# Index keys of a sparse attention kept twice, padded with zeros, so that one product of 128 rows and 512 columns serves two heads

## The chip, the cores and the metric

The kernel runs on one core of a Trainium2 chip. The metric is the time of one execution on the device, in microseconds (us), lower is better. The core has five engines with a queue of instructions each: TensorE (PE, matrix products; its weight loads are listed as PEld), VectorE (DVE), ScalarE (ACT), GpSimd (POOL) and SyncE (SP, which issues the transfers from memory). Each works through its own queue in order, and they wait for one another by semaphores.

## The reference

Two layers with three sublayers each: a feed-forward, a mixer, a feed-forward. For 256 tokens of width 1024, each sublayer computes `x <- LayerNorm(alpha * x + (1 + gate) * f(x * (1 + scale) + shift))`. The mixer of the first layer joins a sparse attention with a gated delta rule. The sparse attention has an index that picks the keys which each query may see:

```python
dots = jnp.einsum('bqhd,bsd->bqhs', iqb, ik32) * IDX_DIM ** -0.5     # 8 index heads of 64, one key of 64 for all
score = jnp.einsum('bqh,bqhs->bqs', iwb, jax.nn.relu(dots))          # weighted sum over the heads
score = jnp.where(visible, score, NEG_INF)
_, sel = lax.top_k(score, top_k)                                     # the 64 best keys of each query
```

The delta rule needs, for each chunk of 64 tokens and each of 4 heads, the inverse of a triangular matrix, and then carries a state from chunk to chunk.

## The kernel before

The tokens lie in two blocks of 128 (`NB`). Weights are split into a high and a low part, and a product of weights and activations is three products in fp32r (`mm3`, L263 to L265). Products inside the mixer, those of the index among them, are in plain float32.

The class `Hybrid` holds the mixer of the first layer. Its `run` projects in turn z, the index key and the gates' inputs (`use_ik`), and the queries, keys and values of the delta rule. Then comes `gdn`, the delta rule: its inversion goes up by levels (L1269 to L1284), with the two token blocks in turn. Each level multiplies on PE (L1272), copies the product to SBUF on ACT (L1274), and multiplies twice more (L1277 and L1281), after which DVE subtracts from the inverse so far (L1282, L1284). Behind it, in the program's text, come the index queries (`use_iq`) and `index`.

For each block, `index` multiplies the 128 queries of a head with the 256 keys. A head has 64 rows, so two heads lie above each other in `iqT` (128 rows, four pairs). The key stands twice in `ikd`, in rows 0 to 63 and in rows 64 to 127, so that each of the two heads has it in its own half of the array (L1060). Two pairs fill two PSUM banks of 512 columns, one bank for the upper heads and one for the lower. ACT takes the Relu of a bank (L1064), DVE multiplies by the head's weight and adds (L1068), and then finds the 64th best score in eight steps (L1072, L1073) and turns it into a bias (L1075, L1076).

A scheduler orders the instructions of each engine ahead of time: it lays instructions that are ready between those that wait, so that products of the index and of later projections stand between those of the delta rule. It also decides which semaphores an instruction waits for. A tile in SBUF can lie where an earlier tile lay; its first writer then waits for the last users of the earlier one. Tiles of the mixer are allocated one behind the other in the pools `hyb` and `hyb1`.

Two more places matter. `gates` (L1134) takes the exponential of `alog`, which is loaded from memory, into the tile `gea`; ACT has to load the table of this function first. And `epilogue` closes the sublayer ahead of the mixer: it normalises x in pieces on ACT (L405) and DVE (L407), PE transposes them (L282), ACT and DVE scale, shift and split the result (L298, L258, L259) into `uT`, and `uT` is what the z projection multiplies first.

Of the kernel before, what the change touches and what calls it, by code (L numbers as in the profile page):

```python
# [11 lines left out]
F32 = mybir.dt.float32  # L12
F32R = mybir.dt.float32r
I32 = mybir.dt.int32
AF = mybir.ActivationFunctionType
ALU = mybir.AluOpType
AX = mybir.AxisListType

P = 128
D = 1024  # L20
KD = D // P
S = 256
# [11 lines left out]
class Trunk:  # L34
# [804 lines left out]
    def run(self, subs):  # L839
        nc = self.nc  # L840
        self.subs = subs
        self.mdone = set()
        self.count = 0
        self.marks, self.last_mm = [None], None
        self.left = None
        goals = (44, 64, 98, 132, 136, 144)
        self.setup()
        self.lead = 0
        self.bg = self.mod_gen()
        self.need(0, 1)  # L850
        self.count += next(self.bg)
        todo = self.todo = [self.sublayer(si, l, j) for si, (l, j) in enumerate(subs)]
        self.make_u(0, self.x, range(NB))
        self.rest = self.setup_rest()
        for si, (l, j) in enumerate(subs):
            last = si == len(subs) - 1
            self.lead = 2 if j == 1 else 0
            self.si, self.base, self.goal = si, self.count, goals[si]
            for _ in todo[si]:
                pass  # L860
            self.need(si, 2)
            self.early, self.gb = [], None
            if not last:
                self.need(si + 1, 0)
                next(todo[si + 1])
            self.load_gb(l, j)
            self.epilogue(si, self.acc, last)
            self.left = self.residual()
            if not last and self.gb is None and subs[si + 1] != (0, 1):
                with self.behind(*self.marks):  # L870
                    for _ in self.left:
                        pass
# [42 lines left out]
class Hybrid:  # L915
# [19 lines left out]
    def run(self):  # L935
        T, nc, one, pool, w = self.T, self.nc, self.one, self.pool, self.w
        zs = T.proj_tok(self.wz, 512, True)
        with T.behind(*T.marks):
            self.constants()
        self.ikd = one.tile([P, S], F32, name="ikd")  # L940
        self.iw = one.tile([P, NB, 8], F32, name="iw")
        self.ab = one.tile([P, NB, 8], F32, name="ab")
        T.proj_t(pool, w, (2048, 72, 3656, 8), 80, self.use_ik)
        gates = self.gates(zs)
        next(gates)
        self.qkv = {}
        for i in range(6):
            if i == 1:
                with T.behind(self.T.recent):
                    for _ in T.left:  # L950
                        pass
            if i == 3:
                for _ in gates:
                    pass
            T.proj_t(pool, w, 2120 + 256 * i, 256, self.use_qkv, (None, nc.gpsimd))
        self.gdn()
        self.iqT = self.tl(one, [P, 4, S], "iqT")
        for i in range(2):
            T.proj_t(pool, w, 1536 + 256 * i, 256, self.use_iq, (nc.gpsimd,))
        self.index()  # L960
        self.aqT = self.tl(one, [P, 4, S], "iqT")
        self.akT = one.tile([P, 4, S], F32, name="akT")
        self.av = one.tile([P, NB, 8, self.DH], F32, name="av")

        def part(g):
            T.proj_t(pool, w, 256 * g, 256, self.use_aq, (nc.gpsimd,))
            self.beat()
            T.proj_t(pool, w, 512 + 256 * g, 256, self.use_ak, (nc.gpsimd,))
            self.beat()
            pts = T.proj_tok(T.tok_load(pool, w, 1024 + 256 * g, 256), 256, False)  # L970
            for b in range(NB):
                nc.scalar.copy(self.av[:, b, 4 * g : 4 * g + 4].rearrange("p h d -> p (h d)"), pts[b][:, 0:256])
            self.beat()

        part(0)
        first = self.dsa(0)
        part(1)
        mix = self.tl(T.wp, [P, 2, KD, S], "uT", F32R)
        op = OutProj(T, pool, "hl", 4, T.t["hyb_w_out"][0], mix)
        self.gdn_out(mix)  # L980
        T.attended(pool, *first, mix, 0)
        second = self.dsa(1, {0: (4,), 1: (5,), 2: (6, 7), 3: (0, 1)}, op)
        T.attended(pool, *second, mix, 2)
        with T.behind(T.turned):
            T.preload(AF.Silu, second[1][:, 1, 3:4])
        for k in (2, 3):
            op.ready(k)
        op.finish(HYBRID_LATE, (2, 3))
        return op.acc
# [25 lines left out]
    def use_ik(self, c, pt):  # L1015
        nc, T = self.nc, self.T
        kw = self.tl(self.pool, [P, S], "k1", bufs=4)
        nc.scalar.copy(kw[0:80], pt[0:80])
        nc.vector.tensor_copy(self.ikd[0:64], pt[0:64])
        nc.vector.tensor_copy(self.ikd[64:128], pt[0:64])  # L1020
        for b in range(NB):
            p2 = T.bank("acc")
            nc.tensor.transpose(p2[:, 0:80], kw[0:80, b * P : (b + 1) * P], T.ident[0:80, 0:80])
            nc.vector.tensor_scalar_mul(self.iw[:, b], p2[:, 64:72], 8.0 ** -0.5)
            nc.vector.tensor_copy(self.ab[:, b], p2[:, 72:80])
# [24 lines left out]
    def index(self):  # L1050
        nc, T = self.nc, self.T
        self.bias = []
        for b in range(NB):
            sc = self.tl(self.one, [P, S], f"sc{b}")
            for hq in range(2):
                pts = [T.bank("acc") for _ in range(2)]
                for i in range(2):
                    for r in range(2):
                        rr = slice(64 * r, 64 * r + 64)
                        nc.tensor.matmul(pts[r][:, i * S : (i + 1) * S], self.iqT[rr, 2 * hq + i, b * P : (b + 1) * P],  # L1060
                                         self.ikd[rr], start=True, stop=True)
                for r in range(2):
                    rl = self.tl(self.pool, [P, 512], "PT")
                    nc.scalar.activation(rl, pts[r], AF.Relu, scale=0.125)  # L1064
                    for i in range(2):
                        h = 4 * hq + 2 * i + r
                        wc = self.iw[:, b, h : h + 1]
                        nc.vector.scalar_tensor_tensor(sc, rl[:, i * S : (i + 1) * S], wc, T.mneg[b] if h == 0 else sc,  # L1068
                                                       ALU.mult, ALU.add)
            for _ in range(8):  # L1070
                m8 = self.tl(self.pool, [P, 8], "m8")
                nc.vector.max(m8, sc)  # L1072
                nc.vector.match_replace(sc, m8, sc, -3e38)  # L1073
            bias = sc
            nc.vector.tensor_scalar(bias, sc, -2e38, NEG, ALU.is_gt, ALU.mult)  # L1075
            nc.vector.tensor_tensor(out=bias, in0=bias, in1=T.nd[b], op=ALU.add)  # L1076
            self.bias.append(bias)
# [460 lines left out]
```

## Time and profile before

| | |
|---|---|
| time of three runs | 1206.98 us median, 1205.5 to 1210.03 |
| profiled execution | 1209.47 us, its span 1207.7 us |
| granted clock of PE, mean | 0.982 |
| PE busy | 94% of the span, 7703 instructions |
| DVE busy | 76% |
| ACT busy | 45% |
| POOL busy | 21% |
| index products, L1060 | 32 instructions of 428 ns, 333.4 to 359.3 us |

Times in the profile count from the start of the span. A matmul's record holds its way through the array, so records of neighbours overlap, and a busy PE is not a PE at its peak. The index and the inversion of the delta rule fill the stretch from 333 to 363 us; the epilogue ahead of the mixer runs from 224 to 245 us.

### The profile page before, as it was taken

What the parts mean: (1) busy time and instruction counts of PE and PEld (TensorE: products, weight loads), DVE (VectorE), ACT (ScalarE), POOL (GpSimd) and SP (SyncE); (2) the same over time, 40 slices, a digit from 0 to 9 for tenths busy, and PEclk for the clock granted to TensorE, in tenths of its full rate; (3) what the DMA queues carried; (4) which work ended last, traced back from release to release, by engine and by line L of the source; (5) the groups of instructions that cost most, each with busy time, mean ns of one, the idle gap of its engine ahead of it and who ended that gap; (6) DMA issues with size and microseconds to landing.
All of it is one profiled execution on the core that took longest, in us unless ns stands there. A gap on an engine that the chain in (4) does not pass through costs nothing.

```text
span 1207.7 us, 19560 instructions
## 1 busy us (share of the span) xinstructions
PE 1131.0 (94%) x7703; PEld 1025.9 (85%) x7703; DVE 917.7 (76%) x1404; ACT 548.5 (45%) x963; POOL 259.4 (21%) x186
## 2 busy tenths in 40 slices
PE   4998999998899998999999999999989998999997
PEld 3887999788787887989999899898988877899995
DVE  6699777698986677878775889767789748866545
ACT  0645444456433445543543543434347656544430
POOL 0631000224731452320000342000122234300001
PEclk9998999999999999999999899999989999999999
DMA  9879998453310576789987488888733335885620
GB/s 354 266 252 342 299 327 299 139 179 119 97 36 5 188 270 218 238 293 320 311 298 248 134 284 283 270 278 298 250 122 102 139 105 190 294 253 185 211 71 35
DMA packets 155333, 259.74 MB, mean 215 GB/s; under 512 B 8813, under 2 KB 117354, under 8 KB 155242
## 3 DMA queue, kind: packets, MB, share of 16 engines
q1 hardware_dynamic: 155050, 258.45, 64.4%
q8 instruction: 60, 0.98, 0.3%
q14 instruction: 31, 0.25, 0.1%
q10 hardware_dynamic: 192, 0.05, 0.0%
HBM read 257.43 MB, written 1.05 MB: 214 GB/s over the span
## 4 chain that ended last, share of the span: by engine, by line
PE 51%; DVE 23%; DMA 13%; issue 5%; ACT 4%; POOL 3%; SPq 0%; POOLq 0%; DVEq 0%; ACTq 0%
PE gu L265 8%; PE gu L263 8%; PE gu L264 8%; PE acc L265 6%; PE acc L264 6%; PE acc L263 6%; DMA wd<-ffn_w_down 5%; DMA wd<-mod_w 4%; DVE macc L225 3%; DMA w<-ffn_w_up 2%; DVE g L259 2%; DVE x L383 1%; POOL hd L259 1%; DMA w<-mod_w 1%; DVE u L259 1%
## 5 line engine op out<-in xcount | busy, mean ns | idle before, releaser
L225 DVE SCALAR_TENSOR_TENSOR macc<-wd,csT,macc 128x1024 f32<-128x1024 f32 x112 | 171.5, 1531 | 28.6 <-DMA wd<-mod_w 28.0
L265 PE MATMUL gu<-uT,g 128*128 128x256 f32 x640 | 181.3, 283 | 1.6 <-DVE g L259 1.6
L263 PE MATMUL gu<-uT,g 128*128 128x256 f32 x640 | 181.2, 283 | 1.3 <-ACT sg L548 1.3
L265 PE MATMUL gu<-uT,u 128*128 128x256 f32 x640 | 181.3, 283 | 1.0 <-DVE u L259 1.0
L263 PE MATMUL gu<-uT,u 128*128 128x256 f32 x640 | 181.2, 283 | 0.0
L264 PE MATMUL gu<-uT,u 128*128 128x256 f32 x640 | 181.1, 283 | 0.0
L264 PE MATMUL gu<-uT,g 128*128 128x256 f32 x640 | 181.1, 283 | 0.0
L258 ACT CAST hd<-wd 128x1024 fp32r<-128x1024 f32 x88 | 92.3, 1049 | 136.8 <-DMA wd<-ffn_w_down 118.8
L263 PE MATMUL acc<-hd,h 128*128 128x512 f32 x352 | 141.5, 402 | 0.5 <-ACT h L258 0.5
L265 PE MATMUL acc<-hd,h 128*128 128x512 f32 x352 | 138.0, 392 | 1.8 <-DVE h L259 1.8
L264 PE MATMUL acc<-hd,h 128*128 128x512 f32 x352 | 138.1, 392 | 0.0
L259 DVE TENSOR_TENSOR g<-w,g 128x1024 fp32r<-128x1024 f32 x86 | 117.0, 1364 | 23.9 <-ACT g L258 23.8
L263 PEld LDWEIGHTS gu<-uT,g 128*128 128x128 f32 x640 | 122.7, 192 | 3.2 <-ACT sg L548 1.8
L265 PEld LDWEIGHTS gu<-uT,g 128*128 128x128 f32 x640 | 122.7, 192 | 2.2 <-DVE g L259 2.2
L264 PEld LDWEIGHTS gu<-uT,g 128*128 128x128 f32 x640 | 122.7, 192 | 1.4
L265 PEld LDWEIGHTS gu<-uT,u 128*128 128x128 f32 x640 | 122.9, 192 | 1.2 <-DVE u L259 1.2
L264 PEld LDWEIGHTS gu<-uT,u 128*128 128x128 f32 x640 | 122.9, 192 | 0.0
L263 PEld LDWEIGHTS gu<-uT,u 128*128 128x128 f32 x640 | 122.9, 192 | 0.0
L259 DVE TENSOR_TENSOR u<-w,u 128x1024 fp32r<-128x1024 f32 x81 | 106.6, 1321 | 20.1 <-ACT u L258 20.0
L259 POOL TENSOR_TENSOR hd<-wd,hd 128x1024 fp32r<-128x1024 f32 x32 | 89.6, 2806 | 137.9 <-ACT hd L258 137.9
L258 ACT CAST u<-w 128x1024 fp32r<-128x1024 f32 (+1 forms) x89 | 91.7, 1038 | 58.1 <-DMA w<-ffn_w_up 44.8
L259 POOL TENSOR_TENSOR hl<-w,hl 128x1024 fp32r<-128x1024 f32 x28 | 72.5, 2602 | 202.0 <-ACT hl L258 201.5
(403 smaller groups left out, 2477.6 us busy)
## 6 DMA issues: line engine op xcount, KB each, us to landing
wd<-mod_w SPq DMA_DIRECT2D x130, 512.0 KB, 4.8
wd<-ffn_w_down SPq DMA_DIRECT2D x88, 512.0 KB, 4.6
w<-ffn_w_gate SPq DMA_DIRECT2D x43, 1024.0 KB, 8.4
w<-ffn_w_up SPq DMA_DIRECT2D x43, 1024.0 KB, 6.3
w<-hyb_w_in SPq DMA_DIRECT2D x16, 1024.0 KB, 6.1
w<-mod_w SPq DMA_DIRECT2D x7, 1024.0 KB, 7.5
w<-hyb_w_out SPq DMA_DIRECT2D x4, 1024.0 KB, 5.0
w<-mla_w_out SPq DMA_DIRECT2D x4, 1024.0 KB, 5.1
```

What stands on the lines that cost most here:

```text
L225: step = nc.vector.scalar_tensor_tensor(acc, w, c, acc, ALU.mult, ALU.add)
L258: i = self.nc.scalar.copy(hi, src)
L259: return i, (eng or self.nc.vector).tensor_tensor(out=lo, in0=src, in1=hi.bitcast(F32), op=ALU.subtract)
L263: nc.tensor.matmul(out, lh, rh, start=first, stop=False)
L264: nc.tensor.matmul(out, lh, rl, start=False, stop=False)
L265: self.last_mm = nc.tensor.matmul(out, ll, rh, start=False, stop=last)
L383: V.tensor_tensor(out=x[:, b, sl], in0=tmp, in1=x[:, b, sl], op=ALU.add)
```

## The change

The key tile becomes `ik2`, twice as wide: its first 256 columns hold the key in rows 0 to 63 and zeros below, its second 256 columns hold zeros above and the key in rows 64 to 127. POOL writes the zeros once. A product now takes all 128 rows of a pair of heads and all 512 columns, and its result has the upper head in the first half of one bank and the lower head in the second half. There is one product for each pair and block, a Relu behind each, and the heads are added in the order 0 to 7.

```diff
-        self.ikd = one.tile([P, S], F32, name="ikd")
+        self.ik2 = one.tile([P, 2, S], F32, name="ik2")
+        for r in range(2):
+            nc.gpsimd.memset(self.ik2[64 - 64 * r : 128 - 64 * r, r], 0.0)
...
-        nc.vector.tensor_copy(self.ikd[0:64], pt[0:64])
-        nc.vector.tensor_copy(self.ikd[64:128], pt[0:64])
+        nc.vector.tensor_copy(self.ik2[0:64, 0], pt[0:64])
+        nc.vector.tensor_copy(self.ik2[64:128, 1], pt[0:64])
...
-            for hq in range(2):
-                pts = [T.bank("acc") for _ in range(2)]
-                for i in range(2):
-                    for r in range(2):
-                        rr = slice(64 * r, 64 * r + 64)
-                        nc.tensor.matmul(pts[r][:, i * S : (i + 1) * S], self.iqT[rr, 2 * hq + i, b * P : (b + 1) * P],
-                                         self.ikd[rr], start=True, stop=True)
+            for p in range(4):
+                pt = T.bank("acc")
+                nc.tensor.matmul(pt, self.iqT[:, p, b * P : (b + 1) * P], self.ik2.rearrange("p a b -> p (a b)"),
+                                 start=True, stop=True)
+                rl = self.tl(self.pool, [P, 512], "PT")
+                nc.scalar.activation(rl, pt, AF.Relu, scale=0.125)
                 for r in range(2):
-                    rl = self.tl(self.pool, [P, 512], "PT")
-                    nc.scalar.activation(rl, pts[r], AF.Relu, scale=0.125)
-                    for i in range(2):
-                        h = 4 * hq + 2 * i + r
...
+                    h = 2 * p + r
...
```

On PE, in the inversion, the order before is this; L1060 stands for one product of 64 rows, and two of them, one for each half of the array, follow each other between L1272 and L1277.

```order
L1060 MATMUL acc_3740<-ikd,iqT_3618 128x256
L1060 MATMUL acc_3741<-ikd,iqT_3618 128x256
L1277 MATMUL gu_3338<-decT_488_3336,tok_480_3303 128x128 x4
L1281 MATMUL gu_3343<-tok_480_3303,decT_488_3336 128x128 x4
L1272 MATMUL gu_3352<-dec_476_3291,vn_3350 128x128 x4
L1060 MATMUL acc_3740<-ikd,iqT_3618 128x256
L1060 MATMUL acc_3741<-ikd,iqT_3618 128x256
L1277 MATMUL gu_3359<-decT_493_3357,tok_477_3292 128x128 x4
```

In the changed kernel the same place reads as follows; its lines are numbered two less here, so L1059 is the index product, and L1275, L1279 and L1270 are the former L1277, L1281 and L1272.

```order
L1059 MATMUL acc_3742<-ik_2510,iqT_3620 128x512
L1275 MATMUL gu_3340<-decT_488_3338,tok_480_3305 128x128 x4
L1279 MATMUL gu_3345<-tok_480_3305,decT_488_3338 128x128 x4
L1270 MATMUL gu_3354<-dec_476_3293,vn_3352 128x128 x4
L1059 MATMUL acc_3748<-ik_2510,iqT_3620 128x512
L1275 MATMUL gu_3361<-decT_493_3359,tok_477_3294 128x128 x4
```

One product of 128 rows and 512 columns stands where the pair stood, in each of the eight rounds; the products around it are the same in the same order.

On ACT, at the end of the feed-forward ahead of the mixer, the order before has the table load free of waits; the names in brackets are the queues whose semaphores an instruction waits for, DMAHW6_49 being that of the transfer of `alog`.

```order
L258 CAST hl_2322<-w_296_2320 128x1024 [waits DMAHW5_49]
L258 CAST hl_2325<-w_296_2320 128x1024
L1134 ACT_TABLE_LOAD
L1134 ACTIVATE gea_2595<-alog 128x4 [waits DMAHW6_49]
L405 ACTIVATE x_118<-x_118,rs_2342 128x256 [waits DVE_49]
L405 ACTIVATE x_118<-x_118,rs_2342 128x256
```

In the changed kernel the same six instructions stand in the same order (L1132 is the former L1134).

```order
L258 CAST hl_2322<-w_296_2320 128x1024 [waits DMAHW5_49]
L258 CAST hl_2325<-w_296_2320 128x1024
L1132 ACT_TABLE_LOAD [waits DMAHW6_49,DVE_49]
L1132 ACTIVATE gea_2597<-alog 128x4 [waits PE_49]
L405 ACTIVATE x_118<-x_118,rs_2342 128x256 [waits DVE_49]
L405 ACTIVATE x_118<-x_118,rs_2342 128x256
```

The wait for the transfer has moved from the exponential to the table load ahead of it, and two waits have come, for DVE and PE instructions of the feed-forward.

On DVE, at the end of the inversion, the order before is this; `sc_563` and `sc_580` are the scores of the first and the second token block, `dec_476` and `dec_479` the inverses of the two blocks.

```order
L1068 SCALAR_TENSOR_TENSOR sc_580_3794<-PT_3815,iw,sc_580_3794 128x256
L1282 TENSOR_TENSOR dec_476_3291<-dec_476_3291,gu_3485 128x512
L1075 TENSOR_SCALAR sc_563_3739<-sc_563_3739 128x256
L1068 SCALAR_TENSOR_TENSOR sc_580_3794<-PT_3819,iw,sc_580_3794 128x256
L1076 TENSOR_TENSOR sc_563_3739<-sc_563_3739,nd_956 128x256
L1068 SCALAR_TENSOR_TENSOR sc_580_3794<-PT_3819,iw,sc_580_3794 128x256
L1072 MAX m_589_3823<-sc_580_3794 128x8
L1282 TENSOR_TENSOR dec_479_3302<-dec_479_3302,gu_3500 128x512
```

And in the changed kernel (again two lines less):

```order
L1066 SCALAR_TENSOR_TENSOR sc_580_3792<-PT_3813,iw,sc_580_3792 128x256
L1280 TENSOR_TENSOR dec_476_3293<-dec_476_3293,gu_3487 128x512
L1073 TENSOR_SCALAR sc_563_3741<-sc_563_3741 128x256
L1066 SCALAR_TENSOR_TENSOR sc_580_3792<-PT_3813,iw,sc_580_3792 128x256
L1074 TENSOR_TENSOR sc_563_3741<-sc_563_3741,nd_956 128x256
L1070 MAX m_589_3817<-sc_580_3792 128x8
L1071 MATCH_REPLACE sc_580_3792<-m_589_3817,sc_580_3792 128x256
L1070 MAX m_590_3820<-sc_580_3792 128x8
L1280 TENSOR_TENSOR dec_479_3304<-dec_479_3304,gu_3502 128x512
```

Between the last two subtractions from the inverse there is one accumulation of scores less, and one step of the search more.

## Rows read from the trace of the kernel before

**Rows 1.** The page: busy time, share of the span and instructions of each engine.
```profile
PE 1131.0 (94%) x7703; PEld 1025.9 (85%) x7703; DVE 917.7 (76%) x1404; ACT 548.5 (45%) x963; POOL 259.4 (21%) x186
```

**Rows 2.** The chain of waits from 333 us: start us, length us, what.
```profile
333.44 0.63 PE acc L1060 x4
...
337.04 0.59 ACT decT L1274
337.68 1.16 PE gu L1277 x8
...
340.71 0.59 ACT decT L1274
```

**Rows 3.** Timeline of PE, second round: start us, length, engine, line, operation, tiles, count.
```profile
336.67 0.28 PE L1272 MATMUL gu<-dec,vn 128*128 128x128 f32 x1
336.87 0.49 PE L1060 MATMUL acc<-ikd,iqT 64*128 64x256 f32 x2
337.19 0.38 PE L1060 MATMUL acc<-ikd,iqT 64*128 64x256 f32 x2
337.68 0.38 PE L1277 MATMUL gu<-decT,tok 128*128 128x128 f32 x1
```

**Rows 4.** Index products by line (busy us, mean ns); L180 in the timeline.
```profile
L1060 PE MATMUL acc<-ikd,iqT 64*128 64x256 f32 x32 | 5.6, 428 | 0.0
...
401.76 0.59 PE L180 MATMUL gu<-macc,one 128*128 128x512 f32 x1
401.76 1.02 PE L180 MATMUL gu<-macc,one 128*128 128x512 f32 x2
```

**Rows 5.** End of the inversion in the timeline; the search's maximum by line.
```profile
364.74 0.67 DVE L1282 TENSOR_TENSOR dec<-dec,gu 128x512 f32<-128x512 f32 x1
365.46 0.97 PEld L1289 LDWEIGHTS gu<-vb,dec 128*128 128x128 f32 x8 [0.20 <-DVE dec L1282]
...
L1072 DVE MAX8 m<-sc 128x8 f32<-128x256 f32 x16 | 6.8, 426 | 0.4
```

**Rows 6.** POOL by line (a fill, a copy); timeline of PE and POOL near 222 us.
```profile
masks.py:197 POOL MEMSET ident<- 128x128 f32 x1 | 0.2, 204 | 0.3 <-POOLq L1527 0.3
...
L1456 POOL COPY kt<-rkT 64x256 f32<-64x256 f32 x8 | 5.0, 676 | 0.1
...
221.50 0.39 PE L265 MATMUL acc<-hd,h 128*128 128x512 f32 x1
...
223.44 5.23 POOL L259 TENSOR_TENSOR hl<-w,hl 128x1024 fp32r<-128x1024 f32 x2 [127.47 <-ACT hl L258]
```

**Rows 7.** Timeline of the epilogue ahead of the mixer; in brackets idle time before, and releaser.
```profile
225.28 1.28 ACT L1134 ACT_TABLE_LOAD   x1
...
234.60 0.21 ACT L1134 ACTIVATE gea<-alog 128x4 f32<-128x4 f32 x1 [8.04 <-DMA alog<-gdn_a_log]
...
235.27 1.09 ACT L405 ACTIVATE x<-x,rs 128x256 f32<-128x256 f32 x2 [0.46 <-DVE rs L400]
...
235.92 1.15 PE L282 MATMUL gu<-ident,x 128*128 128x128 f32 x8 [1.80 <-ACT x L405]
...
237.90 0.50 PE L263 MATMUL acc<-hl,uT 128*128 128x512 f32 x1 [0.83 <-ACT uT L258]
...
239.89 0.76 DVE L259 TENSOR_TENSOR uT<-v,uT 128x256 fp32r<-128x256 f32 x2
...
240.37 0.51 PE L265 MATMUL acc<-hl,uT 128*128 128x512 f32 x1 [0.22 <-DVE uT L259]
```

**Rows 8.** Windows: length, busy us of PE, PEld, DVE, ACT, POOL, PEclk, DMA share, GB/s.
```profile
237.00:240.00 3.00, 2.17 (x9) 1.35 (x8) 2.22 (x9) 3.00 (x10) 0.82 (x2) 1.00 1.04 261
...
676.00:680.00 4.00, 2.24 (x13) 1.92 (x14) 3.23 (x12) 2.86 (x9) 0.81 (x2) 0.95 0.42 131
680.00:684.00 4.00, 3.44 (x17) 3.14 (x16) 2.20 (x7) 2.23 (x6) 0.00 (x0) 0.50 0.01 4
684.00:688.00 4.00, 4.00 (x26) 4.00 (x25) 3.46 (x7) 3.89 (x9) 0.58 (x1) 0.70 0.00 0
```

More of the change, by code (lines that the diff above doesn't have):

```diff
@@ L1054, in index @@
             sc = self.tl(self.one, [P, S], f"sc{b}")
-            for hq in range(2):
-                pts = [T.bank("acc") for _ in range(2)]
-                for i in range(2):
-                    for r in range(2):
-                        rr = slice(64 * r, 64 * r + 64)
-                        nc.tensor.matmul(pts[r][:, i * S : (i + 1) * S], self.iqT[rr, 2 * hq + i, b * P : (b + 1) * P],
-                                         self.ikd[rr], start=True, stop=True)
-                for r in range(2):
-                    rl = self.tl(self.pool, [P, 512], "PT")
-                    nc.scalar.activation(rl, pts[r], AF.Relu, scale=0.125)
-                    for i in range(2):
-                        h = 4 * hq + 2 * i + r
-                        wc = self.iw[:, b, h : h + 1]
-                        nc.vector.scalar_tensor_tensor(sc, rl[:, i * S : (i + 1) * S], wc, T.mneg[b] if h == 0 else sc,
-                                                       ALU.mult, ALU.add)
+            for p in range(4):
[4 more added lines that the diff above has]
+                nc.scalar.activation(rl, pt, AF.Relu, scale=0.125)
+                for r in range(2):
+                    h = 2 * p + r
+                    wc = self.iw[:, b, h : h + 1]
+                    nc.vector.scalar_tensor_tensor(sc, rl[:, r * S : (r + 1) * S], wc, T.mneg[b] if h == 0 else sc,
+                                                   ALU.mult, ALU.add)
             for _ in range(8):
```

## Prediction

> **What bounds the kernel now.** I read the page first: TensorE (PE) is busy 94% of the span [rows 1]. A share over the whole span does not say what the changed lines are worth, so I went to the chain of waits over the stretch where they run, 333 to 363 us. In that chain the reader is to see a pattern that comes back every 3.67 us: L1277, L1281 and L1272 on PE, then a copy on ScalarE (ACT, L1274, 0.59 us), then L1277 again [rows 2]. This is the inversion in the delta rule, in which each product needs the copy of the one before. The index products of L1060 stand in the chain once only, in the first round, for 0.63 us; in the other seven rounds their place is taken by the copy. So they run in the hole that PE has while ACT copies.
>
> The timeline of PE in steps of 0.05 us shows that hole in the second round [rows 3]. The last of L1272 starts at 336.67. L1060 follows at 336.87, two instructions together (0.49 us for both), and two more at 337.19 that end at 337.57. L1277 could not come sooner than its 337.68, since it needs the copy, which the chain has from 337.04 to 337.63 [rows 2]. A float32 product is two instructions here, so one group is two products of 64 rows, one in each half of the array, side by side: each instruction lasts 0.43 us [rows 4], but four take 0.70 us and not 1.7.
>
> **The change part by part.** *The product.* Eight groups of two half-array products (32 instructions) become eight products of 128 rows and 512 columns (16 instructions). The trace has that shape in L180: one instruction takes 0.59 us and two take 1.02, so they follow each other at 0.43 us [rows 4]. So a group grows from 0.70 to 1.02 us, and over eight groups PE's records grow by 8 x 0.32 = 2.6 us. The change does not halve PE's work, it adds to it, because the two halves already ran at the same time.
>
> Here a rule speaks against the change. The Trainium skill, page "TensorEngine Tiling (Array Packing)", section "The Solution", lets a contraction of at most 64 rows run as two independent tiles, up to twice as fast; padding with zeros gives that up. The two starts together in [rows 3] agree with it. The same page, section "Key Properties", says that changing the tiling mode drains TensorE, which speaks for the change; what that would give is the fourth rival.
>
> What of the 2.6 us is on the path? The new product starts at 336.78 if it follows L1272 as instructions of one form do (0.11 us apart: L1277's eight take 1.16 us [rows 2], the first alone 0.38 [rows 3], which leaves 0.78 for seven steps), else at 336.87. Its two instructions hold the array for 2 x 0.43 us, to 337.64 or 337.73. L1277 begins at 337.68 with its weights, and its first product, recorded 0.10 us longer than the others (0.38 against 0.28 us), really streams from about 337.78. So the hole holds it, with 0.05 to 0.14 us to spare. In seven rounds I put it at 0; the ends are 0 (the copy bounds the round, so nothing is gained) and 0.32 us a round, 2.2 us. In the first round L1060 is on the chain, and 0.63 becomes 0.86 us less the 0.08 us by which it starts sooner: +0.15 us.
>
> *ScalarE and VectorE in the index.* The counts and shapes stay: eight Relus of 512 columns, sixteen accumulations of 256. Only their order moves: a Relu now follows each product instead of two after every second one. Each stands ahead of a copy L1274 in ACT's queue, and that could hold up the chain; but the product ends at about 337.9, the Relu 0.6 us later, and the next copy on ACT starts at 340.71 [rows 2], over 2 us later. VectorE (DVE) finishes the first block's scores sooner, and at the end of the inversion this counts a little: L1282 started at 364.74, behind index work, and PE's L1289 waited 0.20 us for it [rows 5]. In the new order the second block's accumulations run one product ahead, and a search step stands in their place; the L1282 of the round before, and with it this one, should come sooner. I take -0.20 us, the whole wait; the other end is +0.4, if the search step only comes on top (its maximum alone is 0.43 us [rows 5]).
>
> *The zeros.* Two fills of 64x256 on GpSimd (POOL). The nearest rows are a fill of 128x128 (0.20 us) and a copy of 64x256 (0.68 us) [rows 6], so both together take 0.4 to 1.4 us. They wait for a product near the end of the feed-forward, the second of five tiles in the first bank, which ends at 221.9, and ahead of them POOL had been idle for 127 us. Behind them is the split of the z weights, which started at 223.44 only when ACT had cast [rows 6]. The gap is 1.5 us: cost 0. At the upper end, with no cover, it is the start of the z projection, at 237.9, that would move, which the 5.2 us of splits leave 9 us free.
>
> *Memory.* The keys take 1 KB more in each partition, so every tile allocated after them in that pool moves. Everywhere but once the waits stay what they were. The exception is gea (L1134, the decay rates): it now lies on a place that the feed-forward used, so its instruction has two waits more, and two of its three were put on the table load in front of it. Before, the table load ran at 225.28, with ACT otherwise idle, and only gea waited until 234.60 for the transfer of a_log [rows 7]. Now the table load itself waits for that transfer, and its 1.28 us come after it: 234.60 + 1.28 + 0.2 = 236.08. Behind it on ACT is L405, the normalising of x at the end of the feed-forward, which started at 235.27: 0.8 us late. For L405 PE's transposes wait (L282, idle 1.80 us [rows 7]), and for ACT's next casts the z projection (idle 0.83 us). So PE's first z product moves from 237.90 to 238.7. Not all of this lasts: six products later, at 239.52 and now 240.32, come two more of 0.23 us, then one that began at 240.37 because it waited 0.22 us for DVE's uT of 239.89. That uT stands on DVE behind work which is not late, so it does not move; the product now starts at 240.78, 0.41 us later than before. From there to 247.9 PE waits for nothing. I take +0.41 us. The ends are 0 (the table load is not held back) and 0.8.
>
> *Elsewhere.* SyncE issues the same transfers in the same order. In the delta rule's state steps six fill-in products move from the waits of the chain to a later place where PE is full: PE does the same work, 0.
>
> Sum: +0.15 - 0.20 + 0.41 = **+0.36 us**. The profiled execution took 1209.47 us (span 1207.7), 2.5 us over the median of 1206.98; on it the sum gives 1209.8, on the median **1207.3 us**. No change that can be measured: 0.5%, about what a measurement of this kernel can tell from none, is 6.0 us.
>
> **The rivals.** *The pause in the epilogue drops PE's clock (slower).* In the epilogue of another sublayer the granted clock was 0.95 while PE was busy 2.24 of 4 us, and then 0.50 and 0.70 for 4 us each, half speed for much of them [rows 8]. From 237 to 240 PE is busy 2.17 of 3 us, and the clock is at 1.00. The change makes exactly this pause 0.8 us longer. It decides if the clock falls before the z products, which then go at 1.2 GHz. The price is what full speed lost there: 4 x 0.50 + 4 x 0.30 = 3.2 us, so 1207.3 + 3.2 = 1210.5 us. For it: the pattern is the same. Against it: with PE's waits of 1.80 and 0.83 us [rows 7] the clock held, and 0.8 us more is a part of that. The Trainium skill, page "TensorE: Matmul & The Clock Gate", section "Why this matters for your kernels", warns of idle gaps between bursts for this reason; the 0.50 after the busy 2.24 agrees.
>
> *The hole is too small.* If the product needs its whole 1.02 us before L1277 can start, each of the other seven rounds is up to 0.32 us longer: 1207.3 + 2.2 = 1209.5 us. Against it: L1277's instructions start 0.11 us apart, though each lasts 0.28 us, so a product does not wait for the end of the one before.
>
> *The table load is not late.* If the waits act on gea alone, 0.41 us go: 1206.9 us.
>
> *The forms of products cost more than I see.* L1060 starts 0.20 us after the last of L1272, where 0.11 is usual: a change of form costs 0.09 us. If all sixteen changes were on the path, 16 x 0.09 = 1.4 us would go: 1207.3 - 1.4 = 1205.9 us. Against it: the copy, not PE, ends each round. (This is the drain of the page named above; the 0.09 us agrees with it.)
>
> **How the numbers follow.** The forecast has 0.62, the clock 0.14, the small hole 0.08, the table load 0.08, the forms 0.08. All five lie within 6 us of 1207.0, so within 0.5% has 0.93; I leave 0.04 for slower (clock and hole together, 5.7 us over the median, and a run a little long) and 0.03 for faster. The cases span 1205.9 to 1210.5, and the three runs before spread from 1205.5 to 1210.03 by themselves: the range is 1204.6 to 1210.8.
>
> **What would show it.** The new product as two instructions of about 0.59 us, 0.43 apart, and rounds that still last 3.67 us from copy to copy. The table load at 234.6, L405 at 236.1, the first z product at 238.7, and the clock still 1.00 from 237 to 246. L1289 without its wait of 0.20 us. If the rounds come out at 3.8 us or more, the hole was too small; if the stretch from 333 to 363 becomes shorter by more than 1 us, I have the bound of the inversion wrong.

## The result, and the profile after

The changed kernel took 1213.92 us (median of six runs, 1212.27 to 1216.77), the kernel before 1207.54 us in the same comparison. The ratio is 1.0053, 95% interval 1.0035 to 1.0072: slower by 6.4 us, and outside the range that was forecast. The profiled execution has a span of 1211.2 us, against 1207.7.

The page hardly differs; its line of the engines answers to [rows 1].

```profile
PE 1132.5 (94%) x7687; PEld 1026.7 (85%) x7687; DVE 921.5 (76%) x1404; ACT 548.0 (45%) x963; POOL 260.7 (22%) x188
```

The stretch that I argued about most is as I had it. These are the chain of waits of the changed kernel in the inversion, answering to [rows 2] (start us, length us, what), and its timeline of PE in the second round, answering to [rows 3].

```profile
342.10 0.86 PE acc L1059 x2
342.96 1.03 PE gu L1275 x8
343.98 0.89 PE gu L1279 x8
344.88 0.89 PE gu L1270 x8
345.77 0.86 PE acc L1059 x2
```

```profile
341.93 1.02 PE L1059 MATMUL acc<-ik,iqT 128*128 128x512 f32 x2
342.83 0.38 PE L1275 MATMUL gu<-decT,tok 128*128 128x128 f32 x1
```

A round still takes 3.67 us (342.10 to 345.77). In this chain the product stands in the copy's place, two instructions of 0.43 us, because PE is now busy up to L1275. But the copy still ends the round:

```profile
342.19 0.58 ACT L1272 COPY decT<-gu 128x512 f32<-128x512 f32 x1 [1.41 <-PE gu L1270]
...
342.82 0.97 PEld L1275 LDWEIGHTS gu<-decT,tok 128*128 128x128 f32 x8 [0.70 <-ACT decT L1272]
```

The weight load of L1275 waits for the copy and starts 0.05 us behind its end (342.77), as it does before (337.62 and 337.67). The product's second instruction starts at 342.36 and takes 0.43 us of the array, to 342.79: the hole holds it with 0.03 us to spare. By line the product has 593 ns, 16 times:

```profile
L1059 PE MATMUL acc<-ik,iqT 128*128 128x512 f32 x16 | 8.2, 593 | 0.0
```

From the first L1270 to the last L1275 the inversion is as long as before, within 0.1 us. The second group of L1287, the former L1289 of [rows 5], has lost its wait of 0.20 us: no bracket stands behind it.

```profile
370.37 0.97 PEld L1287 LDWEIGHTS gu<-vb,dec 128*128 128x128 f32 x8
```

So the loss lies ahead of all that. In the epilogue ahead of the mixer the timeline of the kernel before has these lines beside those of [rows 6, 7]: the reciprocal root on POOL (rs, L118 and L119), DVE's two splits of z weights (hl), and L400, for which L405 waits. The root ends at 231.15 here, 3.9 us before L400 starts, which stands behind the splits in DVE's queue.

```profile
230.28 0.23 POOL L118 TENSOR_SCALAR rs<-mv 128x1 f32<-128x1 f32 x1 [1.60 <-DVE mv L386]
230.58 0.57 POOL L119 TENSOR_TENSOR rs<-rs,mhalf 128x1 f32<-128x1 f32 x1
...
232.82 2.34 DVE L259 TENSOR_TENSOR hl<-w,hl 128x1024 fp32r<-128x1024 f32 x2
...
235.08 0.15 DVE L400 SCALAR_TENSOR_TENSOR rs<-mv,rs 128x1 f32<-128x1 f32 x1
```

And the same place in the changed kernel, where the brackets name idle time ahead and its releaser:

```profile
226.82 0.69 DVE L381 SCALAR_TENSOR_TENSOR tmp<-acc,G 128x512 f32<-128x512 f32 x1 [1.25 <-PE acc L265]
...
231.16 0.39 PE L265 MATMUL acc<-hd,h 128*128 128x512 f32 x1
...
231.66 0.67 POOL L942 MEMSET ik<- 64x256 f32 x2 [135.57 <-DVE x L383]
...
232.29 6.88 DVE L259 TENSOR_TENSOR hl<-w,hl 128x1024 fp32r<-128x1024 f32 x2
...
232.30 4.65 POOL L259 TENSOR_TENSOR hl<-w,hl 128x1024 fp32r<-128x1024 f32 x2
...
234.13 1.28 ACT L1132 ACT_TABLE_LOAD   x1 [9.39 <-DMA alog<-gdn_a_log]
...
236.92 1.19 POOL L118 TENSOR_SCALAR rs<-mv 128x1 f32<-128x1 f32 x1
...
238.19 1.40 POOL L119 TENSOR_TENSOR rs<-rs,mhalf 128x1 f32<-128x1 f32 x1
239.63 0.16 DVE L400 SCALAR_TENSOR_TENSOR rs<-mv,rs 128x1 f32<-128x1 f32 x1 [0.46 <-POOL rs L119]
...
239.82 1.09 ACT L405 ACTIVATE x<-x,rs 128x256 f32<-128x256 f32 x2 [4.20 <-DVE rs L400]
...
240.48 1.97 PE L282 MATMUL gu<-ident,x 128*128 128x128 f32 x8 [6.89 <-ACT x L405]
...
242.70 0.80 PE L263 MATMUL acc<-hl,uT 128*128 128x512 f32 x1 [0.26 <-ACT uT L258]
```

The two fills (L942) ran at 231.66, not at 221.9. The bracket names DVE's L383, which ended at that moment, but what they wait for is the product of L265 that ends at 231.55: in the run with the fills alone (below) they start 0.03 us before L383 ends, and the trace names L265. POOL takes its queue in order, so its two splits came behind them, at 232.30 instead of the 223.44 of [rows 6], and the reciprocal root behind those, at 236.92 instead of 230.28. L400 needs it, L405 needs L400, and PE's transposes stood idle for 6.89 us instead of the 1.80 of [rows 7]. The chain of waits shows the same in one column. In the kernel before it goes through DVE's splits here, and POOL comes on it at 238.24 only, with a later root:

```profile
232.82 2.34 DVE hl L259 x2
```

In the changed kernel POOL is on it from the fills to 239.60.

```profile
232.03 0.30 POOL ik L942
232.33 4.62 POOL hl L259 x2
236.95 1.17 POOL rs L118
...
238.19 1.41 POOL rs L119
...
239.63 0.17 DVE rs L400
```

To compare executions I count from DVE's L381 on the feed-forward's second bank, which PE releases and nothing here touches: it starts at 227.36 us before and at 226.82 after. This is how far behind it three points come in each run, in us: L400, the first z product, and the first L386 of the next sublayer (472.63 before, 477.55 after).

| kernel | L400 | first z product | next L386 |
|---|---|---|---|
| before | 7.72 | 10.54 | 245.27 |
| changed | 12.81 | 15.88 | 250.73 |
| changed, second profile | 12.81 | 15.89 | 251.32 |
| fills behind the epilogue | 7.73 | 11.58 | 246.73 |
| tile in its own place | 7.73 | 10.55 | 245.23 |
| wider tile alone | 7.72 | 11.31 | 247.04 |
| fills alone | 13.02 | 16.10 | 251.18 |
| tiny fills alone | 12.61 | 15.69 | 251.01 |
| changed, small products in the pause | 12.82 | 15.65 | 250.21 |
| changed, wide products in the pause | 12.82 | 15.64 | 250.16 |
| late fills, each product twice | 7.72 | 11.57 | 253.33 |
| own place, root first | 3.38 | 9.76 | 253.03 |

The first z product of the changed kernel is 5.34 us late; 5.09 of it are in L400, and the other 0.25 come in behind it, where the transposes took 1.97 us instead of 1.15, at a granted clock that had fallen to 0.50 (windows as in [rows 8]):

```profile
237.00:240.00 3.00, 0.00 (x0) 0.00 (x0) 2.54 (x4) 0.18 (x1) 2.51 (x2) 0.75 0.19 43
240.00:243.00 3.00, 2.26 (x9) 1.87 (x10) 2.97 (x10) 2.71 (x8) 0.21 (x1) 0.50 1.10 261
243.00:246.00 3.00, 3.00 (x9) 2.37 (x9) 1.76 (x7) 3.00 (x10) 0.74 (x2) 0.61 0.96 338
```

The wait of the table load came as forecast, 234.13 instead of 225.28, but cost nothing, since L405 now waits until 239.82 for something else.

### The profile page after: what moved, and what is told of

Same layout as the page of the kernel before. It is cut to its first block, busy times and chain, and to the rows that moved or that the text cites. A ratio compares the mean times of both kernels' runs of the same rounds, so it can differ in the third digit from the quotient of the medians.

```text
span 1211.2 us, 19530 instructions
## 1 busy us (share of the span) xinstructions
PE 1132.5 (94%) x7687; PEld 1026.7 (85%) x7687; DVE 921.5 (76%) x1404; ACT 548.0 (45%) x963; POOL 260.7 (22%) x188
## 4 chain that ended last, share of the span: by engine, by line
PE 57%; DVE 22%; DMA 9%; issue 4%; ACT 4%; POOL 3%; SPq 0%; POOLq 0%; DVEq 0%; ACTq 0%
PE gu L265 9%; PE gu L263 9%; PE gu L264 9%; PE acc L265 7%; PE acc L263 7%; PE acc L264 6%; DMA wd<-ffn_w_down 4%; DVE macc L225 3%; DMA wd<-mod_w 3%; DVE u L259 2%; DVE g L259 2%; DVE x L383 1%; DMA w<-mod_w 1%; PE gu L770 1%; DVE G L225 1%
## 5 line engine op out<-in xcount | busy, mean ns | idle before, releaser
L265 PE MATMUL gu<-uT,g 128*128 128x256 f32 x640 | 181.3, 283 | 1.7 <-DVE g L259 1.7
L265 PE MATMUL gu<-uT,u 128*128 128x256 f32 x640 | 181.3, 283 | 1.0 <-DVE u L259 1.0
L265 PE MATMUL acc<-hd,h 128*128 128x512 f32 x352 | 137.6, 391 | 2.1 <-DVE h L259 2.1
L265 PEld LDWEIGHTS gu<-uT,g 128*128 128x128 f32 x640 | 122.7, 192 | 2.4 <-DVE g L259 2.4
L265 PEld LDWEIGHTS gu<-uT,u 128*128 128x128 f32 x640 | 122.8, 192 | 1.2 <-DVE u L259 1.2
L259 DVE TENSOR_TENSOR hd<-wd,hd 128x1024 fp32r<-128x1024 f32 x56 | 69.7, 1248 | 42.5 <-ACT hd L258 42.3
```

Source lines behind the costliest of these rows:

```text
L259: return i, (eng or self.nc.vector).tensor_tensor(out=lo, in0=src, in1=hi.bitcast(F32), op=ALU.subtract)
L265: self.last_mm = nc.tensor.matmul(out, ll, rh, start=False, stop=last)
```

## The experiments

Theory F: the fills wait in POOL's queue for the feed-forward, and the splits and the reciprocal root behind them are late. Rival P: the products of 512 columns cost the time. Rival L: the wider tile moves its neighbours, and the table load's wait costs it. The line numbers of each run are its own.

**The fills behind the epilogue.**

```diff
-        for r in range(2):
-            nc.gpsimd.memset(self.ik2[64 - 64 * r : 128 - 64 * r, r], 0.0)
+        with T.behind(*T.marks):
+            for r in range(2):
+                nc.gpsimd.memset(self.ik2[64 - 64 * r : 128 - 64 * r, r], 0.0)
```

> The changed kernel, with the two fills of zeros ordered behind the end of the feed-forward's epilogue instead of in front of the split of the z weights; products, copies and the double-width tile stay. Theory F (the fills wait in POOL's queue for a bank of the feed-forward, and the z weights' split and the reciprocal root of the epilogue wait behind them): the split starts at about 223.4 us as before, L405 at 235.3 to 235.7, the z product's first PE matmul at 237.9 to 238.4, and the time is that of the kernel before, 1207.3 to 1208.2 us. Rival P (the products over 128 rows and 512 columns, and the hole that they have to fit, cost the 6 us): nothing is regained, about 1213.9 us. Rival L (the double-width tile moves the other buffers, the table load waits for a transfer, and that costs the 6 us): also about 1213.9 us.

1207.91 us, ratio to the kernel before 0.9998, interval 0.9986 to 1.0011: all of the loss is gone, with the products and the wider tile still there. That is against P and L. Its timeline:

```profile
224.00 5.22 POOL L259 TENSOR_TENSOR hl<-w,hl 128x1024 fp32r<-128x1024 f32 x2 [128.02 <-ACT hl L258]
...
230.82 0.23 POOL L118 TENSOR_SCALAR rs<-mv 128x1 f32<-128x1 f32 x1 [1.61 <-DVE mv L386]
...
235.22 1.28 ACT L1133 ACT_TABLE_LOAD   x1 [9.40 <-DMA alog<-gdn_a_log]
...
236.62 1.08 ACT L405 ACTIVATE x<-x,rs 128x256 f32<-128x256 f32 x2
...
239.71 0.83 POOL L943 MEMSET ik<- 64x256 f32 x2
```

POOL's order is that of before again, and the fills run at 239.71 in nobody's way. L405 now waits for the table load, 1.28 us that end at 236.50, as the forecast had it, though the expectation of this run had left it out; L400 is as early as before, and the first z product is 1.04 us late in the table, which the time does not show.

**The fills alone, on the old products.**

```diff
-        self.ikd = one.tile([P, S], F32, name="ikd")
+        ik2 = one.tile([P, 2, S], F32, name="ik2")
+        self.ikd = ik2[:, 0]
+        for r in range(2):
+            nc.gpsimd.memset(ik2[64 * r : 64 * r + 64, 1], 0.0)
```

> The kernel before with its products of half an array, plus the double-width tile and two fills of 64 rows and 256 columns on POOL at the place where the changed kernel has them; their zeros are read by nobody. Theory F: all of the loss is here, 1213 to 1214.3 us; the fills run near 231.7 us, the POOL split behind them starts near 232.3, the z product near 242.7. Rival P: the time of before, 1207.5 us. Rival L: about 1213.9 us as well.

1215.58 us, ratio 1.0069, interval 1.0056 to 1.0083: the whole loss without one changed product. The fills began at 232.42, while L383 ran until 232.45, and here the trace names PE's L265 as what released them; the first z product is 5.6 us late, against 5.3 in the changed kernel.

```profile
232.42 0.67 POOL L943 MEMSET ik<- 64x256 f32 x2 [136.43 <-PE acc L265]
...
233.17 6.61 POOL L259 TENSOR_TENSOR hl<-w,hl 128x1024 fp32r<-128x1024 f32 x2
```

That is 8.3 us over the kernel before (6.8 to 10.0), where I had given 5.5 to 6.8; what the surplus is stays open (below).

**A place of its own for the tile.**

```diff
-        self.ik2 = one.tile([P, 2, S], F32, name="ik2")
+        self.ik2 = T.const.tile([P, 2, S], F32, name="ik2")
```

> The changed kernel with the double-width tile in a place of its own, so that no fill waits for an earlier user of it, and the fills run at the start of the program; the other buffers lie as before and the table load has no wait for a transfer. Theory F: 1207.2 to 1207.9 us, POOL's split at 223.4 and the z product at 237.9. Rival P: 1213.9 us. Rival L: 1207.5 us, so this run against the one with late fills tells L from F.

1207.12 us, ratio 0.9990, interval 0.9978 to 1.0002. The fills now wait for no other stage and stand at the start of the program, at 0.98 and 1.62, and the first z product is where it was.

```profile
0.98 0.31 POOL L942 MEMSET ik<- 64x256 f32 x1
```

No run here is faster than the kernel before; this one and the late fills are level with it.

**The wider tile alone**, the edit of the run with the fills alone, without its fills.

> The kernel before with its products, plus the double-width tile alone: no fills, and the second half is written by nobody. The table load then waits for the transfer of alog. Theory F: the table load ends at about 235.4 instead of 226.6 and L405 starts 0.2 to 0.8 us later than 235.27: 1207.5 to 1208.3 us. Rival L: about 1213.9 us. Rival P: 1207.5 us.

1209.99 us, ratio 1.0014, interval 1.0002 to 1.0027. L is refuted: the first z product is 0.77 us late, the forecast's own figure for this step, not 5.3. The ratio is 1.7 us over the kernel before (0.2 to 3.3), where 0.8 had been computed; the interval holds that.

```profile
234.67 1.28 ACT L1135 ACT_TABLE_LOAD   x1 [9.39 <-DMA alog<-gdn_a_log]
...
236.08 1.08 ACT L405 ACTIVATE x<-x,rs 128x256 f32<-128x256 f32 x2
```

**Tiny fills**, on the old products: the same wait, one column each.

```diff
-            nc.gpsimd.memset(ik2[64 * r : 64 * r + 64, 1], 0.0)
+            nc.gpsimd.memset(ik2[64 * r : 64 * r + 64, 1, 0:1], 0.0)
```

> The run with the fills alone, but each fill covers one column instead of 256: same wait, hardly any length. Theory F (it is the wait in POOL's queue that costs): the fills still run near 231.7 us, the split behind them starts 0.5 us earlier than with long fills at most, the z product at 242.5 to 243.5, and the time is 1213.5 to 1216 us. Rival D (the fills' own duration or their writing costs): back to the time of before with the wider tile, 1208 to 1210 us.

1213.30 us, ratio 1.0060, interval 1.0036 to 1.0085. The wait costs, not the length: 0.24 us of filling instead of 0.67 leave the first z product 5.2 us late.

```profile
231.53 0.24 POOL L943 MEMSET ik<- 64x1 f32 x2 [136.25 <-PE acc L265]
...
231.85 5.65 POOL L259 TENSOR_TENSOR hl<-w,hl 128x1024 fp32r<-128x1024 f32 x2
```

**The clock.** The changed kernel with products that nobody reads on PE in the pause, first 24 of 128x128, then seven of 128x512 (shown):

```diff
+        if si == 0:
+            with self.behind(self.last_mm):
+                for _ in range(7):
+                    nc.tensor.matmul(self.bank("gu"), self.ident, G[:, 0:512], start=True, stop=True)
```

> The changed kernel with 24 products of 128x128 whose results nobody reads, on PE in the pause of that epilogue, behind the feed-forward's last product, so that PE is busy until about 240 us. Theory F with the clock as a part of it: the granted clock stays at 1.00 from 237 to 246 where it was 0.50 to 0.75, the z products follow each other at 0.23 instead of 0.43 us, and 1.5 to 3 us of the 6 come back: 1211 to 1212.5 us. Rival C (the whole loss is the clock): 1207.5 to 1208.5 us. Rival N (the clock costs nothing since transfers end this stretch anyway): 1213.9 us.

> The changed kernel with seven products of 128x512 on PE in the pause of the first sublayer's epilogue, whose results nobody reads, in place of the 24 of 128x128: about 7 x 0.86 = 6 us, from 234 to 240, up to the transposes. In the run with the small ones the clock fell to 0.50 at 243 nevertheless, so that the clock's share of the loss stayed open. If it holds at 1.00 from 237 to 249 now: theory with the clock as a part, z products 0.23 us apart instead of 0.43 and the end of the token projections 1 to 2 us sooner, 1211 to 1212.5 us against the changed kernel of the same call at 1213.9; theory N (transfers end that stretch anyway), no difference from it. If it falls again, the clock's share cannot be told by this means.

> The changed kernel once more, word for word, as the partner on the same chip for the run with wide products and for the clock in a second profile: 1213 to 1214.5 us, the fills near 231.7 to 232.5 us, the pause of PE 6.9 us, and the clock at 0.50 behind it.

With the small ones 1210.46 us, ratio 1.0032, interval 1.0018 to 1.0046, but the clock fell all the same: 0.97 from 240 to 243 and 0.50 from 243 to 246. With the wide ones 1211.60 us, 1.0035, interval 1.0021 to 1.0049, and the clock held:

```profile
237.00:240.00 3.00, 2.98 (x7) 0.95 (x6) 2.56 (x2) 0.00 (x0) 2.90 (x3) 1.00 0.08 14
240.00:243.00 3.00, 1.31 (x9) 1.00 (x10) 2.98 (x10) 2.75 (x7) 0.00 (x0) 1.00 1.10 239
243.00:246.00 3.00, 2.72 (x11) 1.86 (x12) 1.90 (x8) 3.00 (x10) 0.78 (x2) 1.00 1.05 363
```

The changed kernel again beside it took 1213.63 us, 1.0045, interval 1.0031 to 1.0060. The intervals of all three overlap, so the 1 to 2 us between their ratios are not shown. In the table the next sublayer comes 0.5 to 1.2 us sooner than in the two profiles of the changed kernel, but just as much sooner in the run in which the clock did fall at 243. So theory N, that the clock costs nothing here, is not excluded: by these profiles the clock's share is about 1 us at most, while the times alone would leave room for more. Rival C, the clock as the whole loss, is out: with the clock at 1.00 the kernel is still slower, and without the wait in the queue all of the loss is gone.

**Each index product twice**, in the run with late fills, into the same bank, with half the scale in the Relu.

```diff
-                nc.tensor.matmul(pt, self.iqT[:, p, b * P : (b + 1) * P], ..., start=True, stop=True)
+                for n in range(2):
+                    nc.tensor.matmul(pt, self.iqT[:, p, b * P : (b + 1) * P], ..., start=n == 0, stop=n == 1)
```

> The run with late fills, with each index product issued twice into the same bank and the scale of the Relu halved. Theory H (the new product of 2 x 0.43 us just fills the hole that PE has while ACT copies): each of the eight rounds of the inversion becomes about 0.86 us longer, 3.67 to 4.5 us, together 6 to 7 us: 1213.9 to 1214.8 us. Rival W (the hole is wide, the products are off the path altogether): 1207.9 us. If the hole were too small already, a round would also be longer by 0.86, but the rounds of the changed kernel would be longer than before too, which they are not (3.67 us both).

1215.52 us, ratio 1.0074, interval 1.0056 to 1.0092. The loss, 8.9 us over the kernel before (6.8 to 11.1), came near the 6 to 7 us expected, but by luck, for the place was wrong. The scheduler laid one product in each of the eight holes, whose rounds stayed at 3.67 us (339.35 to 343.02 in its chain), and the other eight between the state steps behind the inversion, where PE has no hole; there they should cost 8 x 0.86 = 6.9 us, and the table has the next L386 6.6 us behind that of the run with late fills.

```profile
339.35 0.86 PE acc L1061 x2
...
343.02 0.86 PE acc L1061 x2
```

So this run does not measure how wide the hole is. It shows that a product is free in the hole and costs about its full length where PE is full.

**The reciprocal root first.** Since POOL's and DVE's order sets the z product, I tried to gain by it, on the run with the tile in its own place:

```diff
-            with self.behind(*self.early):
+            with self.behind(*(self.early if si else ())):
                 self.marks[0] = self.rsqrt(rs[:, 1:2], mv[:, 1:2], LN_EPS)
```

> The run with the double-width tile in its own place, and in the first sublayer's epilogue the reciprocal root on POOL is no longer ordered behind the splits of the z weights, so that POOL has it in front of them, and DVE's L400 and L407 stand in front of the tail's sums and splits. If what holds the z product up is POOL's and DVE's queue (theory F, applied once more): L400 at about 230.5 instead of 234.1, the transposes L282 right behind the feed-forward's last product, and 0 to 2 us less than 1207.1. If the splits, now later, come too late for the z product: 1207.1 to 1212 us. Which it is I cannot tell from the trace.

1213.57 us, ratio 1.0053, interval 1.0031 to 1.0075, slower than either expectation. L400 and the first z product do come early (3.38 and 9.76 us in the table's count), but the second z product waits 2.47 us for DVE's split of the weights, which now stands behind the sums and statistics of the epilogue (L381 to L384), and the third 3.75 us for the split of uT, which stands behind both. The clock is at 0.50 meanwhile, from 240 to 249.

```profile
230.86 4.72 POOL L259 TENSOR_TENSOR hl<-w,hl 128x1024 fp32r<-128x1024 f32 x2
230.93 2.34 DVE L400 SCALAR_TENSOR_TENSOR rs<-mv,rs 128x1 f32<-128x1 f32 x1 [0.99 <-POOL rs L119]
...
239.01 1.22 DVE L259 TENSOR_TENSOR hl<-w,hl 128x1024 fp32r<-128x1024 f32 x1
...
240.28 0.79 PE L264 MATMUL acc<-hl,uT 128*128 128x512 f32 x1 [2.47 <-DVE hl L259]
244.82 0.79 PE L265 MATMUL acc<-hl,uT 128*128 128x512 f32 x1 [3.75 <-DVE uT L259]
```

## Why the prediction was wrong

**The step that failed** is the one on the zeros: "They wait for a product near the end of the feed-forward, the second of five tiles in the first bank, which ends at 221.9", and from it "The gap is 1.5 us: cost 0". The product is the second of five tiles, but of the last of the four banks. The banks follow each other at 3.4 us (fifteen products at 0.23 us); three banks on from 221.9 is 232.1, and the changed kernel, 0.54 us early at this place, filled at 231.66. I took the bank's place from its name instead of looking for it in PE's timeline. With 232.1 the gap to 223.44 is 8.7 us on the wrong side, and the same paragraph held the rest: behind the fills stands the split, then the reciprocal root. What the prediction put at 0 measured 5.2 to 5.6 us at the first z product (tiny fills, changed kernel, fills alone).

I also wrote that the start of the z projection had 9 us free at the upper end. I counted to the split's own use by PE and missed the reciprocal root, which stands in POOL's queue behind the split: the 9 us were not slack. The slack was that of the root, 3.9 us from its end to L400. Counted from the same L381, the root ended 9.0 us later (239.59 instead of 231.15); less 3.9, that is the 5.1 us of L400.

**A price that no term held** is VectorE and GpSimd side by side. DVE's two splits took 6.88 us in the changed kernel beside POOL's, and 2.34 before, with POOL idle. 2.34 and POOL's 4.65 are 6.99: DVE's first waited for both of POOL's to end, and then DVE worked at its usual pace. POOL's two short instructions of the root, 0.23 and 0.57 us before, took 1.19 and 1.40 beside DVE's splits. The Trainium skill, page "SBUF — State Buffer", section "SBUF: two separate sides", has this as a lock: a VectorE instruction with two inputs in SBUF and a GpSimd one that reads SBUF share a pair of ports, and who starts first holds it for its whole instruction. The lengths agree; who came first can't be told here, since the two start 0.01 us apart. In the run with the fills alone DVE's first split starts 0.07 us ahead of POOL's, and there POOL's is the one that is stretched, to 3.33 us from the 2.36 of the changed kernel. So the queue's delay grew by 1.8 us on POOL alone.

**What held.** The hole: 0 in the rounds, shown by 3.67 us before and after and by the copy, which still ends each of the seven rounds; the room was 0.03 us to L1275's recorded start, or 0.13 as the prediction counts it (0.05 to 0.14), with the 0.10 us by which L1275's first record is longer. L1289's wait went. The table load made L405 0.8 us late, as computed, in the runs with late fills and with the wider tile alone, and was hidden in the changed kernel. The forms of products gave nothing that the rounds show.

**The rival on the clock** was half right. I had it decided by a pause 0.8 us longer. Three runs had just this pause in front of the transposes: with the wider tile alone (2.58 us) the clock stayed at 1.00 to 249, with late fills (2.59 us) and with each product twice (2.58 us) it was 0.50 from 237 to 243. So such a pause sometimes drops it. But the fall did not cost the 3.2 us: from the first z product to the next L386 it was 235.15 us with it and 235.73 without (the differences of the table's columns).

**What stays open.** Kernels with the old products came out about 2 us slower than their partners with the new ones (1.0014 beside 0.9998; 1.0069 beside 1.0053 and 1.0045); the intervals overlap. In the profiles the difference lies far behind the index, between the L386 at 672 us and that at 883: 209.2 to 211.8 us in the four with old products, 205.7 to 209.0 in the eight with new. The order of instructions there is the same in the kernel before and the changed one, so my guess is that the transfers of the weights start at other moments; no run tells.

## What to carry to other kernels

- A small instruction in an engine that is idle isn't free: ask which instruction it waits for, find that one in the timeline by its place in the program and not by its tile's name, and then ask what stands behind it in the same queue, who waits for the last of that, and how much slack that one had.
- A tile that is cut from a reused place brings waits with it. Give a constant that is filled once a place of its own, or order the fill behind the stage whose memory it takes; either gave back all 6 us here.
- Where two products ran side by side in a hole, one padded product that still fits the hole cost nothing and gained nothing here. It would not gain where PE is full either, as far as busy time tells (8.2 us for the padded products against 5.6 for the pairs [rows 4]); no run compares the two there.

## What the runs showed of the hardware that I had not expected

- VectorE stopped by GpSimd in full: in the run with the root first, an instruction of one column (L400, 0.15 us) took 2.34 us when it started 0.07 us behind the first of two POOL splits, which took 4.72 us together.
- The clock fell to 0.50 from 243 to 246 although PE had worked through 24 products of 128x128 until 239.6 us; with seven of 128x512 in the same pause it stayed at 1.00. The transposes came 1.54 us behind the small ones and 0.89 us behind the wide ones, so the runs do not tell if the size or the gap made the difference.
